# Two quarters of the modulation summed on VectorE and GpSimd before TensorE closes them

## The chip, the core and the metric

The kernel runs on one core of one Trainium2 chip. The metric is the device time of one execution in microseconds. Before the change the median of three runs is 1029.71 us (1029.26 to 1030.7). Engine names are those of the profile: PE is TensorE (PEld its weight loads), DVE is VectorE, ACT is ScalarE, POOL is GpSimd, SP is SyncE, which issues most of the DMAs.

## The reference, cut to what matters

One layer of a diffusion transformer, all in float32: 1024 latent tokens (`x`), 256 context tokens (`ctx`), width 1024. Only its beginning is touched:

```python
mod_x = (silu(c) @ w_mod + b_mod)        # one row of 6*1024 for the latents
mod_c = silu(c_ctx) @ w_mod + b_mod      # one row for the context tokens
sh1, sc1, ... = split(mod_x, 6);  csh1, csc1, ... = split(mod_c, 6)
h_x = rmsnorm(x, g_pre_mix) * (1 + sc1) + sh1       # 1024 x 1024
h_c = rmsnorm(ctx, g_pre_mix) * (1 + csc1) + csh1   # 256 x 1024
u_x = h_x @ w_in[:, :512]                           # pool part; then q, k, v, attention, output, MLP
```

Shift and scale of the first sub-layer are a product of a vector of 1024 with a 1024 x 2048 part of `w_mod`, for two vectors at once: silu(c) and silu(c_ctx).

## The kernel before, in words

Products are kept near float32 by splitting each operand into a high part (fp32r) and a low part (what is left), and summing three matmuls: high by high, low by high, high by low. ACT makes the high part and DVE the low part (`high_low`, L181, through L146 or L148 and L152 or L154; `modulated`, L202, with L205 to L210).

The beginning (`startup`, all five engines in the order in which the program is written, by `in_order`, L104) goes in four quarters q of the width, each of 256 columns of shift and 256 of scale, which are two blocks k = 2q and 2q + 1 of 128 rows of the transposed latents `xT`:

- SP loads in this order: eight pages of `x`; then for each quarter four pages of `w_mod` of 512 KB (`mod_load`, L297, issue at L300: K half by shift or scale, each 128 partitions x 4 blocks of K x 256 columns) and the raw rows of `w_in` (`wu0` to `wu3`, L178); then the context tokens. The pages come from a pool of 33, and SP waits only for a DMA eight places earlier.
- `mod_rows(q)` (L409) sums the quarter's modulation on PE: for each of the 8 blocks k of K and each of shift and scale, one matmul of 32 columns of `sT` (column 0 is silu(c), column 1 silu(c_ctx), the rest zero) with 256 columns of `w_mod` (L401), in four column groups of 32 of one bank `pm`: groups 0 and 1 take shift and scale of even k, groups 2 and 3 those of odd k. That is 16 matmuls, 32 records in the profile. ACT copies `pm` to `mrow` (L406).
- `shift_scale(q, mr)` (L415): four records of a small matmul with a constant `pck` turn the rows into columns and add the two halves (L418, `pmt`); DVE adds the bias and multiplies by the gain (L422 to L427, for the latents v = 0 and the context v = 1).
- `latents(q)` (L458) makes `hx`, the modulated latents, high and low, for two halves b of the tokens and the two blocks k: ACT L208, DVE L209 and L210 for b = 0; ACT L205 and L206, DVE L210 for b = 1.
- `some_sums(b, js, k)` (L444, matmuls at L449) adds block k of K to the sums `pu` of the pool part: 12 matmuls for b = 0 and 6 for b = 1 (the other 6 follow later).

The loop over q (the lines that the diff changes stand in it) has for q < 3: the sums of b = 0 with k = 2q, `mod_rows(q + 1)`, the split of the next weights `wu(q + 1)`, the sums of b = 0 with k = 2q + 1, `shift_scale(q + 1)`, the sums of b = 1 with both k, `latents(q + 1)`. So the PE work between the end of `mod_rows` and the first use of the new quarter hides the copy, the turn into columns, the scales and the first `hx`.

GpSimd has nothing to do between the eight reciprocal roots of the token norms (L140, each an operation of one element in a partition) and the two of the context tokens at the end of q = 2. Its other work in the kernel, which the prediction uses for prices, are the attention tables (L885) and a few splits (L896 and L897); L1374, L1387 and L136 to L140 are the norms of a later stage.

Of the kernel before, what the change touches and what calls it, by code (L numbers as in the profile page):

```python
# [11 lines left out]
F32 = mybir.dt.float32  # L12
# [6 lines left out]
P = 128  # L19
D = 1024  # L20
# [60 lines left out]
def hybrid_block(ctx, tc, x, ctx_in, w_mod, b_mod, gp1, gp2, w_in, pool_w, rpb, w_out, w1, w2, vectors,  # L81
                 mask, edge, out):
    nc = tc.nc
    sub, mul, add = ALU.subtract, ALU.mult, ALU.add
# [8 lines left out]
    def cst(name, shape, dt=F32):  # L93
        return const.tile(shape, dt, tag=name, name=name)
# [4 lines left out]
    def page(name, dt=F32):  # L99
        return act.tile([P, 1024], dt, tag="pg", name=name)  # L100
# [75 lines left out]
    def load(name, src):  # L176
        raw = wraw.tile([P, 1024], F32, tag="raw", name=f"{name}w")
        nc.sync.dma_start(raw.rearrange("p (a b) -> p a b", b=src.shape[-1]), src)  # L178
        return raw

    def high_low(name, raw, factor=1.0):  # L181
        hi = whl.tile([P, 1024], F32R, tag="hl", name=f"{name}h")
        lo = whl.tile([P, 1024], F32R, tag="hl", name=f"{name}l")
        split(raw, hi, lo, factor)
        return hi, lo
# [4 lines left out]
    def pair(w, kk, c0, n):  # L190
        return w[2 * kk * P : (2 * kk + 2) * P, c0 : c0 + n].rearrange("(a p) f -> p a f", p=P)

    def wk(w, k, lo, c, n):
        return w[k // 2][lo][:, (k % 2) * 512 + c : (k % 2) * 512 + c + n]
# [70 lines left out]
    def lasting(name):  # L265
        return ps_t.tile([P, 512], F32, tag="T", name=name)
# [4 lines left out]
    with tc.tile_pool(name="ps1", bufs=6, space=PSUM) as ps1, tc.tile_pool(name="tmp1", bufs=3) as tmp:  # L271

        def bank(name):
            if name[:2] == "pm" or name in ("pxt1_0", "pxt0_2", "pxt1_7", "pct2", "pct3"):
                return lasting(name)
            return ps1.tile([P, 512], F32, tag="mm", name=name)

        def once(name, shape):
            return tmp.tile(shape, F32, tag=name, name=name, bufs=1)
# [11 lines left out]
        def token_tile(name, src):  # L291
            t = page(name)
            nc.sync.dma_start(t, src)
            return t


        def mod_load(q, kh, w):  # L297
            src = w_mod[:, w * D + q * 256 : w * D + (q + 1) * 256].rearrange("(h k p) f -> h p k f", p=P, h=2)
            t = page(f"wm{q}_{kh}_{w}")
            nc.sync.dma_start(t.rearrange("p (k f) -> p k f", k=4), src[kh])  # L300
            return t

        xn = [token_tile(f"x{n}", x[n * P : (n + 1) * P, :]) for n in range(NT)]
        wm, raw_u = [], []
        for q in range(4):
            wm.append([[mod_load(q, kh, w) for w in range(2)] for kh in range(2)])
            raw_u.append(load(f"wu{q}", pair(w_in, q, 0, 512)))
        cp = [token_tile(f"c{i}", ctx_in[i * P : (i + 1) * P, :]) for i in range(2)]

# [4 lines left out]
        sT = once("sT", [P, KT, 32])  # L314
# [12 lines left out]
        def squares(name, t):  # L327
            jk = page(f"jk{name}")
            ms = sm(f"ms_{name}", 1, 4)
            mean_square(jk, t, ms)  # L330
            inverse[name] = rsqrt_of(f"t_{name}", ms)

        def normalised(name, t):
            nc.vector.tensor_scalar_mul(t, t, inverse[name])
# [59 lines left out]
        s1 = [cst(f"s1{v}", [P, KT]) for v in range(2)]  # L394

        def mod_sums(q, pm, kh):
            for k in range(4 * kh, 4 * kh + 4):
                for w in range(2):
                    c = 2 * (k % 2) + w
                    o = (k % 4) * 256  # L400
                    nc.tensor.matmul(pm[32 * c : 32 * c + 32, :256], sT[:, k, :], wm[q][kh][w][:, o : o + 256],  # L401
                                     start=(k < 2), stop=(k >= KT - 2))

        def mod_kept(q, pm):
            mr = tmp.tile([P, 256], F32, tag="mrow", name=f"mrow{q}", bufs=2)
            nc.scalar.copy(mr, pm[:, :256])  # L406
            return mr

        def mod_rows(q):  # L409
            pm = bank(f"pm{q}")  # L410
            for kh in range(2):
                mod_sums(q, pm, kh)
            return mod_kept(q, pm)

        def shift_scale(q, mr):  # L415
            pt = bank(f"pmt{q}")
            for j in range(2):
                nc.tensor.matmul(pt[:, 4 * j : 4 * j + 4], mr[:, j * P : (j + 1) * P], pck, start=True, stop=True)  # L418
            pv = pt[:, :8].rearrange("p (j w v) -> p w v j", w=2, v=2)
            hs = slice(2 * q, 2 * q + 2)  # L420
            for v in range(2):
                nc.vector.tensor_tensor(a1[v][:, hs], pv[:, 1, v], b_sc[:, hs], add)  # L422
                nc.vector.tensor_tensor(a1[v][:, hs], a1[v][:, hs], g1c[:, hs], mul)
                if q < 2:
                    nc.vector.tensor_tensor(s1[v][:, hs], pv[:, 0, v], b_sh[:, hs], add)
                else:
                    nc.vector.scalar_tensor_tensor(s1[v][:, hs], pv[:, 0, v], -1.0, b_sh[:, hs], mul, sub)  # L427
# [16 lines left out]
        def some_sums(b, js, k):  # L444
            h = hx[b][k]
            hi, lo = h[:, :512], h[:, 512:]
            for n, (low, r) in enumerate(((0, hi), (1, hi), (0, lo))):
                for j in js:
                    nc.tensor.matmul(pus[b][j], wk(wgt, k, low, j * P, P), r,  # L449
                                     start=(k == 0 and n == 0), stop=(k == KT - 1 and n == 2))  # L450
# [7 lines left out]
        def latents(q):  # L458
            for b in range(2):
                for k in (2 * q, 2 * q + 1):  # L460
                    latent(b, k)
# [5 lines left out]
        pm = bank("pm0")  # L467
        for kh in range(2):
            mod_sums(0, pm, kh)
        mr = mod_kept(0, pm)  # L470
        nc.scalar.copy(wu0h, raw_u[0])
        wgt.append((wu0h, wu0l))
# [10 lines left out]
        for q in range(4):  # L483
            some_sums(0, range(4), 2 * q)
            if q == 0:
                some_sums(0, (0, 1), 1)
            if q < 3:
                mr = mod_rows(q + 1)
                wgt.append(high_low(f"wu{q + 1}", raw_u[q + 1], 1.0 if q == 0 else -1.0))
            some_sums(0, range(2 if q == 0 else 0, 4), 2 * q + 1)  # L490
            if q < 3:
                shift_scale(q + 1, mr)
            for k in (2 * q, 2 * q + 1):
                some_sums(1, range(2), k)
            if q < 3:
                latents(q + 1)
            if q == 2:
                for i, t in enumerate(cp):
                    squares(f"c{i}", t)
                for i, t in enumerate(cp):  # L500
                    normalised(f"c{i}", t)
# [59 lines left out]
        for k in range(KT):  # L561
            for i in range(2):
                o = (k % 2) * 256 + i * P
# [392 lines left out]
        with in_order(ET.PE, ET.Pool, ET.Activation, ET.DVE, ET.SP) as pooling:  # L956
            banks = {of: [bank(f"p{of}{j}") for j in range(2)] for of in "KQ"}
            use(-1)
            for step, (n, of, j) in enumerate([(n, of, j) for n, of in products for j in range(2)]):
                half_product(n, of, j, banks[of])  # L960
                use(step)
                if step in (5, 9, 17):
                    name = {5: "S1", 9: "S4", 17: "S3"}[step]
# [4 lines left out]
                if step in (7, 11):  # L968
                    name = {7: "S4", 11: "S3"}[step]
# [19 lines left out]
    with (  # L989
# [4 lines left out]
        bank = lasting  # L994
# [178 lines left out]
        def halves_of(name):  # L1173
            both = [page(f"{name}{i}") for i in range(2)]
            return [both[t // 2][:, (t % 2) * 512 : (t % 2) * 512 + 512] for t in range(4)]
# [17 lines left out]
        with in_order(ET.PE, ET.Activation, ET.DVE, ET.SP) as projected:  # L1193
# [27 lines left out]
            for i in range(N + 4):  # L1221
# [48 lines left out]
                else:  # L1270

                    t = i - N
                    if t == 0:
                        x, s1 = [], halves_of("so1_")
# [51 lines left out]
    with tc.tile_pool(name="ps2", bufs=6, space=PSUM) as ps2:  # L1326
# [6 lines left out]
      with ExitStack() as tmp2:  # L1333
        tmp = tmp2.enter_context(tc.tile_pool(name="tmp2", bufs=4))
# [20 lines left out]
        def out_bank_sums(name, a, w):  # L1355
            ps = [bank(f"{name}_{t}") for t in range(4)]
            for t in range(4):
                out_sums(ps[t], a, w, t, True)
            return ps
# [32 lines left out]
        with tc.issue_after(projected[ET.DVE]), tc.issue_after(projected[ET.Activation]), in_order(ET.Activation, ET.DVE) as added:  # L1392
# [20 lines left out]
            v = out_bank_sums("pov", "S3", wt3)  # L1413
            c = {}
# [484 lines left out]
        with tc.issue_after(first[ET.PE]), in_order(ET.PE, ET.Activation, ET.DVE, ET.SP):  # L1899
# [3 lines left out]
            tmp = tmp2.enter_context(tc.tile_pool(name="tmp3", bufs=4))  # L1903

            def four(name):
                return [bank(f"{name}_{t}") for t in range(4)]

            def halves(name):
                both = [page(f"{name}{i}") for i in range(2)]
                return [both[t // 2][:, (t % 2) * 512 : (t % 2) * 512 + 512] for t in range(4)]  # L1910
# [19 lines left out]
            def half(m, h):  # L1930
                return rows[m][:, h * 512 : (h + 1) * 512]
# [37 lines left out]
            s1 = halves("s1")  # L1969
# [15 lines left out]
            v, z = four("pyv"), four("pyz")  # L1985
# [10 lines left out]
            for g in range(NG // 2):  # L1996
                group(v, "P4", g, more=True, last=(g == NG // 2 - 1))
                group(z, "P3", g, more=True)
                c = half(4 + g, 1)
# [53 lines left out]
```

## Time and profile before

| what | value |
|---|---|
| median of three runs | 1029.71 us |
| profiled execution, its own time | 1031.34 us |
| its span on the core | 1029.6 us |
| mean granted TensorE clock | 0.996 |
| PE busy | 1014.6 us, 99% |
| DVE busy | 747.1 us, 73% |
| ACT busy | 546.8 us, 53% |
| POOL busy | 142.6 us, 14% |

The profile is that of one execution. A row of the timeline gives the start in us from the beginning of the span, the duration, the engine, the line of the kernel, the operation, output and inputs with their shapes, how many instructions are merged in it, and in square brackets how long the engine had been idle and what ended that. A row of groups gives the busy time in us and the mean duration of one instruction in ns. A row of the windows gives the length of the stretch, the busy time of PE, PEld, DVE, ACT and POOL with their instructions, the granted TensorE clock, the share of the DMA engines and GB/s.

### The profile page before, as it was taken

Reading aid. Unit: us, or ns where it says so; the run is one execution under the profiler, and the core shown is the slowest. Engines: PE = TensorE matmul, PEld = TensorE weight load, DVE = VectorE, ACT = ScalarE, POOL = GpSimd, SP = SyncE. Lnnn points to the kernel's source line nnn. Section 1 sums busy time; section 2 is a strip of 40 time slices with the busy share of each in tenths; the row PEclk is TensorE's granted clock in tenths of the full one; section 3 lists DMA queues with packets and bytes.
Section 4 is the critical chain, followed back from the end, with each engine's and each line's share of the span. In section 5 each row is a group of like instructions: output and inputs, shape, how many; then the busy total and the mean of one; then the engine's idle time right before and its main releaser. Section 6 shows DMA issues by size and latency. Waiting matters only on the chain.

```text
span 1029.6 us, 16022 instructions
## 1 busy us (share of the span) xinstructions
PE 1014.6 (99%) x5910; PEld 840.7 (82%) x5910; DVE 747.1 (73%) x1160; ACT 546.8 (53%) x945; POOL 142.6 (14%) x225
## 2 busy tenths in 40 slices
PE   8999999999999999999999999999999999999997
PEld 7788888878898788888888888888888888888885
DVE  5588757857886687878998888755766666556576
ACT  7573254338897556776655554545543334334431
POOL 3011110126774311410000000000000000000001
PEclk9999999999999999999999999999999999999999
DMA  9999798623338966785776667537967766556556
GB/s 343 333 255 338 248 257 303 204 48 97 74 94 215 214 180 190 262 229 186 260 262 202 216 204 230 189 123 242 337 218 263 254 222 220 201 183 190 172 185 210
DMA packets 123134, 222.70 MB, mean 216 GB/s; under 512 B 9456, under 2 KB 55152, under 8 KB 123056
## 3 DMA queue, kind: packets, MB, share of 16 engines
q1 hardware_dynamic: 96560, 171.14, 50.6%
q0 software_dynamic: 9360, 19.58, 9.4%
q10 hardware_dynamic: 17136, 30.97, 8.1%
q8 instruction: 46, 0.75, 0.3%
q14 instruction: 32, 0.26, 0.1%
HBM read 168.16 MB, written 52.45 MB: 214 GB/s over the span
## 4 chain that ended last, share of the span: by engine, by line
PE 94%; DMA 2%; DVE 1%; issue 0%; ACT 0%; POOL 0%; SPq 0%; DVEq 0%; POOLq 0%; ACTq 0%
PE pu L449 4%; PE pa L1098 4%; PE S L1018 3%; PE phz L198 3%; PE phv L198 3%; PE phx L198 3%; PE pyx L198 3%; PE phx L200 3%; PE pyx L200 3%; PE phz L200 3%; PE pyx L199 3%; PE pyv L198 3%; PE pyz L199 3%; PE pyv L199 3%; PE phv L200 3%; PE pyz L198 3%
## 5 line engine op out<-in xcount | busy, mean ns | idle before, releaser
L1044 ACT ACTIVATE sp<-sp,nm 128x640 f32<-128x640 f32 (+1 forms) x64 | 51.5, 804 | 11.4 <-DVE nm L1033 5.3
L1033 DVE CUSTOM_DVE_ANT_0 sp<-S,tab 128x640 f32<-128x640 f32 (+1 forms) x56 | 44.5, 795 | 14.2 <-PE pz L1064 10.3
L1639 ACT ACTIVATE c<-c 128x512 f32<-128x512 f32 x48 | 30.3, 631 | 44.8 <-DVE c L1759 25.7
L146 ACT CAST wpS<-S 128x512 fp32r<-128x512 f32 x64 | 38.8, 616 | 27.4 <-PE phv L200 9.5
L198 PE MATMUL phx<-thB,wpA 128*128 128x512 f32 x128 | 50.2, 392 | 0.0
L200 PE MATMUL phx<-thB,wpA 128*128 128x512 f32 x128 | 49.8, 389 | 0.0
L199 PE MATMUL phx<-tlB,wpA 128*128 128x512 f32 x128 | 49.8, 389 | 0.0
L152 DVE TENSOR_TENSOR wpS<-S,wpS 128x512 fp32r<-128x512 f32 x64 | 43.4, 685 | 7.4 <-ACT wpS L146 7.4
L140 POOL TENSOR_TENSOR ry<-vy,nhalf 128x1 f32<-128x1 f32 x8 | 5.9, 740 | 281.5 <-DVE vy L138 281.5
L1640 ACT ACTIVATE c<-c 128x512 f32<-128x512 f32 x48 | 30.3, 630 | 15.6 <-DVE sa L1722 12.1
L198 PEld LDWEIGHTS phx<-thB,wpA 128*128 128x128 f32 x128 | 24.0, 188 | 5.4 <-ACT s L1690 0.5
L200 PEld LDWEIGHTS phx<-thB,wpA 128*128 128x128 f32 x128 | 24.0, 188 | 5.1
L199 PEld LDWEIGHTS phx<-tlB,wpA 128*128 128x128 f32 x128 | 24.0, 188 | 4.8
L1098 PE MATMUL pa<-pt,v 128*64 128x128 f32 x352 | 25.9, 280 | 0.2
L1083 DVE COPY pt<-T 128x512 f32<-128x512 f32 x32 | 21.9, 686 | 5.6 <-PE T L1064 5.6
L198 PE MATMUL phz<-thB,wpS 128*128 128x512 f32 x64 | 25.0, 391 | 0.0
L198 PE MATMUL phv<-thT,wpA 128*128 128x512 f32 x64 | 25.0, 391 | 0.0
L199 PE MATMUL phz<-tlB,wpS 128*128 128x512 f32 x64 | 24.9, 390 | 0.0
L199 PE MATMUL phv<-tlT,wpA 128*128 128x512 f32 x64 | 24.9, 389 | 0.0
L200 PE MATMUL phz<-thB,wpS 128*128 128x512 f32 x64 | 24.9, 389 | 0.0
L199 PE MATMUL phy<-tlT,wpS 128*128 128x512 f32 x64 | 24.9, 389 | 0.0
L200 PE MATMUL phy<-thT,wpS 128*128 128x512 f32 x64 | 24.9, 389 | 0.0
(1133 smaller groups left out, 3431.8 us busy)
## 6 DMA issues: line engine op xcount, KB each, us to landing
b<-in_w SPq DMA_DIRECT2D x64, 512.0 KB, 4.6
hrS<-hdS SPq DMA_DIRECT2D x32, 512.0 KB, 5.0
hrA<-hdA SPq DMA_DIRECT2D x24, 512.0 KB, 5.8
wm<-in_w_mod SPq DMA_DIRECT2D x16, 512.0 KB, 9.8
wa_0w<-in_w SPq DMA_DIRECT2D x16, 512.0 KB, 5.0
wa_1w<-in_w SPq DMA_DIRECT2D x16, 512.0 KB, 4.4
hdA<-c ACTq DMA_DIRECT2D x32, 256.0 KB, 2.9
hdS<-sa ACTq DMA_DIRECT2D x32, 256.0 KB, 3.2
```

Source lines behind the costliest of these rows:

```text
L146: nc.scalar.copy(hi, src)
L152: nc.vector.tensor_tensor(lo, src, hi.bitcast(F32), sub)
L198: nc.tensor.matmul(ps, ahi, bhi, start=first, stop=False, skip_group_check=more)
L199: nc.tensor.matmul(ps, ahi, blo, start=False, stop=False, skip_group_check=more)
L200: nc.tensor.matmul(ps, alo, bhi, start=False, stop=last, skip_group_check=more)
L449: nc.tensor.matmul(pus[b][j], wk(wgt, k, low, j * P, P), r, start=(k == 0 and n == 0), stop=(k == KT - 1 and n == 2))
L1018: nc.tensor.matmul(S[e][:, c0 : c0 + k[0].shape[1]], q[n_q][hs, cols], k[n_k][hs], start=(n_q + n_k == 0), stop=(n_q == 1))
L1033: nc.vector.tensor_tensor_reduce(out=to, in0=s, in1=bt, scale=1.0, scalar=BIG, op0=add, op1=ALU.min, accum_out=nm)
L1044: nc.scalar.activation(sp, sp, AF.Exp, bias=least[i, e], scale=-1.0, accum_out=sums[i][:, e : e + 1])
L1098: nc.tensor.matmul(pa[e * HD : (e + 1) * HD, cols], v[:, f : f + HD], turns[i][:, e, c] if c < 4 else fifths[i][:, :, (e + 1) * HD : (e + ...
L1639: nc.scalar.activation(r, src, AF.Relu)
L1640: nc.scalar.activation(r, r, AF.Square)
```

## The change

Quarters 0 and 1 stay as they are. For quarters 2 and 3:

- the weights come as four pages by blocks of K (two blocks each, shift and scale side by side), each in two DMAs of 256 KB (`mod_pairs`), so 8 DMAs of 256 KB in a quarter instead of 4 of 512 KB;
- blocks 0 to 5 of K are multiplied by silu(c) on DVE and by silu(c_ctx) on GpSimd, and added there over the blocks, all 128 partitions apart, shift and scale in one operation of 512 columns (`mod_added`): DVE does one `tensor_scalar_mul` and five `scalar_tensor_tensor`, GpSimd six `tensor_scalar_mul` and five `tensor_tensor` in a quarter;
- PE closes the sum (`mod_closed`): four matmuls for blocks 6 and 7 and four that sum the two added tiles over the partitions with a constant `pick`, eight instead of 16;
- in the loop, blocks 0 and 1 of quarter 2 are added in q = 0 ahead of the split of `wu1`; in q = 1 blocks 2 to 5 of quarter 2 and 0 and 1 of quarter 3 stand ahead of the split of `wu2`; in q = 2 blocks 2 to 5 of quarter 3 stand ahead of the split of `wu3`. `mod_closed` stands behind the sums of b = 0 with k = 2q + 1, where `mod_rows` stood ahead of them, and half of the sums of b = 1 (k = 2q) moves between `mod_closed` and `shift_scale`.

```diff
+        def mod_pairs(q, h):
+            t = page(f"wm{q}_{h}")
+            to = t.rearrange("p (k w f) -> w p k f", k=2, w=2)
+            for w in range(2):
+                src = w_mod[h * 2 * P : (h + 1) * 2 * P, w * D + q * 256 : w * D + (q + 1) * 256]
+                nc.sync.dma_start(to[w], src.rearrange("(k p) f -> p k f", p=P))
+            return t
...
-            wm.append([[mod_load(q, kh, w) for w in range(2)] for kh in range(2)])
+            wm.append([[mod_load(q, kh, w) for w in range(2)] for kh in range(2)] if q < 2 else
+                      [mod_pairs(q, h) for h in range(4)])
...
+        pick = once("pick", [P, 2, 32])
+        nc.gpsimd.memset(pick, 0.0)
+        for v in range(2):
+            nc.gpsimd.memset(pick[:, v, v : v + 1], 1.0)
+        added = {}
+
+        def mod_added(q, ks):
+            if q not in added:
+                added[q] = [tmp.tile([P, 512], F32, tag="t", name=f"md{q}_{v}", bufs=7) for v in range(2)]
+            for k in ks:
+                w = wm[q][k // 2][:, (k % 2) * 512 : (k % 2) * 512 + 512]
+                s0, s1 = (sT[:, k, v : v + 1] for v in range(2))
+                if k == 0:
+                    nc.vector.tensor_scalar_mul(added[q][0], w, s0)
+                    nc.gpsimd.tensor_scalar_mul(added[q][1], w, s1)
+                else:
+                    nc.vector.scalar_tensor_tensor(added[q][0], w, s0, added[q][0], mul, add)
+                    more = tmp.tile([P, 512], F32, tag="t", name=f"mm{q}_{k}", bufs=7)
+                    nc.gpsimd.tensor_scalar_mul(more, w, s1)
+                    nc.gpsimd.tensor_tensor(added[q][1], added[q][1], more, add)
+
+        def mod_closed(q):
+            pm = bank(f"pm{q}")
+            for k in range(2):
+                for w in range(2):
+                    c, o = 2 * k + w, (2 * k + w) * 256
+                    nc.tensor.matmul(pm[32 * c : 32 * c + 32, :256], sT[:, 6 + k, :], wm[q][3][:, o : o + 256],
+                                     start=True, stop=False)
+            for v in range(2):
+                for w in range(2):
+                    c = 2 * v + w
+                    nc.tensor.matmul(pm[32 * c : 32 * c + 32, :256], pick[:, v, :], added[q][v][:, w * 256 : w * 256 + 256],
+                                     start=False, stop=True)
+            return mod_kept(q, pm)
...
             some_sums(0, range(4), 2 * q)
             if q == 0:
                 some_sums(0, (0, 1), 1)
+            if q == 0:
+                mr = mod_rows(q + 1)
+            elif q < 3:
+                mod_added(q + 1, range(2, 6))
+            if q < 2:
+                mod_added(q + 2, range(2))
             if q < 3:
-                mr = mod_rows(q + 1)
                 wgt.append(high_low(f"wu{q + 1}", raw_u[q + 1], 1.0 if q == 0 else -1.0))
             some_sums(0, range(2 if q == 0 else 0, 4), 2 * q + 1)
+            if q in (1, 2):
+                mr = mod_closed(q + 1)
+                some_sums(1, range(2), 2 * q)
             if q < 3:
                 shift_scale(q + 1, mr)
-            for k in (2 * q, 2 * q + 1):
+            for k in (2 * q, 2 * q + 1) if q in (0, 3) else (2 * q + 1,):
                 some_sums(1, range(2), k)
```

The added tiles `md` and the products `mm` share the seven 512-wide slots of tag `t` with the first two `hx` temporaries.

## The prediction

> **What bounds the kernel now.** I read the page first (shares, then the chain that ended last), then the chain, the waits and the windows of the beginning.
>
> ```profile
> span 1029.6 us, 16022 instructions
> PE 1014.6 (99%) x5910; PEld 840.7 (82%) x5910; DVE 747.1 (73%) x1160; ACT 546.8 (53%) x945; POOL 142.6 (14%) x225
> ...
> PE 94%; DMA 2%; DVE 1%; issue 0%; ACT 0%; POOL 0%; SPq 0%; DVEq 0%; POOLq 0%; ACTq 0%
> ```
>
> PE is busy 99% of the span and carries 94% of the chain, so what PE does later or longer in the beginning comes out at the end one to one, unless a later wait for something that does not move gives it back. The stretch of the change, cut from the chain, and the only DMA wait among PE's waits:
>
> ```profile
> 37.01 1.86 PE pm L401 x32
> 38.87 2.95 PE pu L449 x12
> 41.82 0.34 PE pmt L418 x4
> 42.16 5.59 PE pu L449 x24
> 47.75 1.86 PE pm L401 x32
> ```
>
> ```profile
> PEld pm L401 <- DMA wm<-in_w_mod: 0.2, 1, 0.2
> ```
>
> And the stretch in the windows:
>
> ```profile
> 23.20:76.40 53.20, 53.20 (x316) 41.79 (x317) 37.77 (x76) 35.96 (x61) 4.39 (x4) 1.00 0.96 296
> ```
>
> PE works without a gap from 23.2 to 76.4 us; a matmul of `some_sums` costs 5.59 / 24 = 0.233 us there, a round of modulation 1.86 us. DVE is busy 37.8 of those 53.2 us and POOL 4.4. After this stretch PE waits for no DMA, only for engines that follow PE's own work, so I take no part of a delay as given back.
>
> **The change part by part.**
>
> *Removed from PE.* Two rounds of 16 matmuls become two of 8: 2 x 1.86 / 2 = 1.86 us less. This is the whole possible gain.
>
> *Added to DVE and POOL, priced alone.* The nearest rows with the same shape, all operands in SBUF:
>
> ```profile
> L210 DVE TENSOR_TENSOR hx<-xT,hx 128x512 fp32r<-128x512 f32 x14 | 9.4, 690 | 1.4 <-ACT hx L206 1.1
> L209 DVE TENSOR_SCALAR xT<-xT,a,s 128x512 f32<-128x512 f32 x6 | 3.3, 544 | 1.7 <-ACT hx L208 1.7
> L423 DVE TENSOR_TENSOR a<-a,cols 128x2 f32<-128x2 f32 x8 | 1.3, 161 | 0.3
> L154 DVE SCALAR_TENSOR_TENSOR mix<-y,mix 128x512 fp32r<-128x512 f32 x4 | 2.6, 684 | 0.0
> L896 POOL CAST qP<-q 128x512 fp32r<-128x512 f32 x4 | 2.4, 612 | 0.0
> L897 POOL TENSOR_TENSOR qP<-q,qP 128x512 fp32r<-128x512 f32 x4 | 5.2, 1290 | 0.3
> ```
>
> DVE in a quarter: one multiplication at 0.544 (L209) and five `scalar_tensor_tensor` at 0.684 (L154), 3.96 us. POOL: five additions at 1.290 (L897), and six multiplications, whose form has no row. They lie between the one-input cast, 0.612, and the two-input addition, 1.290; I take 0.61, because one tensor comes in as with the cast, and keep 1.29 for the range. That makes 6 x 0.61 + 5 x 1.29 = 10.1 us, against a period of 10.7 us (37.01 to 47.75). Alone, each engine would just keep up. They are not alone.
>
> *DVE and POOL shut each other out.* The rows that decide, from the timeline and the groups:
>
> ```profile
> 203.59 0.45 POOL L885 TENSOR_TENSOR tab<-msk,U0w 128x128 f32<-128x128 f32 x1
> 203.60 1.53 DVE L154 SCALAR_TENSOR_TENSOR wQT4l<-wQT4w,wQT4h 128x1024 fp32r<-128x1024 f32 x1 [0.18 <-ACT wQT4h L148]
> 204.01 1.43 POOL L885 TENSOR_TENSOR tab<-msk,U0w 128x128 f32<-128x128 f32 x1
> L885 POOL TENSOR_TENSOR tab<-msk,U 128x128 f32<-128x128 f32 x36 | 15.1, 450 | 0.0
> L154 DVE SCALAR_TENSOR_TENSOR wu3l<-wu3w,wu3h 128x1024 fp32r<-128x1024 f32 x1 | 1.2, 1225 | 3.4 <-ACT wu3h L148 3.4
> 7.21 0.76 DVE L334 TENSOR_SCALAR x<-x,rt_x 128x1024 f32<-128x1024 f32 x1
> 6.13 0.55 POOL L140 TENSOR_TENSOR rt_x<-vt_x,nhalf 128x1 f32<-128x1 f32 x1 [4.61 <-DVE vt_x L136]
> 7.36 1.02 POOL L140 TENSOR_TENSOR rt_x<-vt_x,nhalf 128x1 f32<-128x1 f32 x1 [0.68 <-DVE vt_x L136]
> ```
>
> A DVE operation with two SBUF inputs, 1.225 us elsewhere, takes 1.53 when it starts just behind a POOL operation; the next POOL operation takes 1.43 instead of 0.45 and ends at 205.44, 0.31 us behind DVE's end at 205.13. So they go one after the other. Behind a DVE `TENSOR_SCALAR` (7.21 to 7.97) the POOL root takes 1.02 instead of 0.55. Of the 0.45 us of the POOL operation, DVE waited 1.53 - 1.225 = 0.31; 0.13 us of each POOL operation are therefore free, and I count the rest as exclusive.
>
> The Trainium skill, SBUF — State Buffer, section "SBUF: two separate sides", says the same of the port pair that the two share, but has the holder keep it for the whole instruction; by that the 22 POOL operations would hold 2.9 us more and the time would be 1049. The 0.31 of 0.45 us here speaks for the smaller value.
>
> *The ledger.* From the landing of quarter 2's first page to POOL's last addition of quarter 3, these operations exclude each other:
> - DVE: the added sums, 2 x 3.96 = 7.92; `latents` of quarters 1 and 2, each 2 x 0.544 (L209) + 4 x 0.690 (L210), 7.70 in all; the low halves of `wu1` to `wu3`, 3 x 1.225 = 3.68 (`wu3`'s follows DVE's last sum at once and so comes ahead of POOL's last addition; 1.2 less if it does not); four gain products at 0.161 (L423), 0.64. Sum 19.9.
> - POOL: in a quarter 6 x (0.61 - 0.13) + 5 x (1.29 - 0.13) = 8.7; two, 17.4.
>
> Together 37.3 us. One of the two always has such an operation ready: when DVE waits for `pmt` or `hx`, POOL still has its chain, and POOL waits for nothing but pages, its own results and slots. (POOL's multiplications for blocks 4 and 5 of quarter 3 also wait until PE has read quarter 2's tiles, which is earlier.) The start:
>
> ```profile
> 21.27 2.01 SPq L300 DMA_DIRECT2D wm<-in_w_mod  x1
> wm<-in_w_mod SPq DMA_DIRECT2D x1, 512.0 KB, 9.9
> ```
>
> This is quarter 2's first page; bytes and order of the queue stay the same, so the new first page (two DMAs) lands at about 21.27 + 9.9 = 31.2 as well; the engines start at 31.3. POOL's last addition ends at 31.3 + 37.3 = 68.6.
>
> *From there to PE's restart.* PE then has the last two pick matmuls (1.86 / 8 = 0.23), six moved matmuls (1.40), `pmt` (0.34) and six more (1.40): 72.0. The chain beside it (the three rows between serve further down):
>
> ```profile
> 32.04 0.15 DVE L422 TENSOR_TENSOR a<-pmt,cols 128x2 f32<-128x2 f32 x1
> 32.49 1.52 ACT L208 ACTIVATE hx<-xT,s,a 128x512 fp32r<-128x512 f32 x2 [1.63 <-DVE s L425]
> 34.12 1.07 PE L449 MATMUL pu<-hx,wu1h 128*128 128x512 f32 x4
> 36.78 0.69 DVE L210 TENSOR_TENSOR hx<-xT,hx 128x512 fp32r<-128x512 f32 x1 [0.38 <-ACT hx L206]
> 30.90 1.23 DVE L152 TENSOR_TENSOR wu1l<-wu1w,wu1h 128x1024 fp32r<-128x1024 f32 x1 [2.63 <-ACT wu1h L146]
> 55.62 1.07 PE L449 MATMUL pu<-hx,wu3h 128*128 128x512 f32 x4
> ```
>
> From DVE's scale to the first `hx` it is 32.49 - 32.04 + 1.52 / 2 = 1.2 us, just covered by the last six matmuls (1.40); before, twelve covered it, so that cover is used up. Before, PE began quarter 3's sums at 55.62. The delay is 72.0 - 55.6 = 16.4 us, with the saved 1.86 already in it, since PE waits for the closing anyway. Half-way the same ledger has on DVE quarter 2's sums (3.96), the first two blocks of quarter 3 (1.23), one `latents` (3.85), two low halves (2.45) and two gain products (0.32), on POOL one quarter (8.7): 20.5 us, so quarter 2 closes at about 52 instead of 37.01 + 1.86 = 38.9.
>
> *Edits with small or no cost.* The first two added blocks stand in DVE's queue from 30.90 - 2.63 = 28.3 until the page lands; queued behind them are `wu1`'s low half and quarter 1's scales. Without any exclusion, scales that came at 32.04 would come at 31.3 + 0.54 + 0.68 + 1.23 = 33.7, and PE, whose sums of k = 2 began at 34.12, 0.9 us after their `hx` (32.49 + 0.76), would stop 0.8 us. In the ledger this is contained. SP issues eight more DMAs; the bytes are the same, PE's whole wait for these pages was 0.2 us, and now they are needed later: nothing. If the smaller DMAs left the queue thin, the start at 31.3 would move with the landing; a late us there is a late us in the ledger. ACT's high parts of `wu2` and `wu3` come ahead of the `mrow` copy, which waits for PE anyway. The three memsets of `pick` fall into POOL's idle time.
>
> *Sum.* Profiled execution: 1031.34 + 16.4 = 1047.7. It lies 1.6 above the median of the runs, so the forecast is 1029.7 + 16.4 = 1046.1. Two corrections I leave out, since they cancel: DVE's rows overlap by some 0.07 us (32.04 begins before the row that ends at 30.90 + 1.23), about 25 times, -1.7; and the clock (rival 4 has the rows), +1.7 for the second of two gaps; behind the first, PE's loss is hidden while POOL works through its second chain. The windows that show it:
>
> ```profile
> 218.00:221.00 3.00, 2.12 (x12) 1.47 (x12) 2.91 (x6) 1.97 (x4) 0.40 (x1) 1.00 1.02 175
> 221.00:224.00 3.00, 2.28 (x16) 1.77 (x15) 3.00 (x6) 1.87 (x4) 0.00 (x0) 0.79 0.66 169
> 224.00:227.00 3.00, 3.00 (x9) 2.11 (x8) 2.68 (x7) 1.50 (x4) 0.00 (x0) 0.64 0.01 3
> ```
>
> **The rivals.**
>
> 1. *No exclusion for these forms* (the other side). Then the 0.8 us stop, and a wait at each closing for DVE, which starts the last four blocks only behind `latents` (36.78 + 0.69 + 1.6 + 4 x 0.684 = 41.8, where PE arrives at 34.9 + 5.59 + 0.46 = 41.0), eat the gain: +0.1 to +0.9, 1030. With none of these waits it is -1.86, 1027.9. It decides where exclusion adds under 1 us a quarter. Against it: the rows at 203.6.
> 2. *Exclusion only between two-input operations.* Seen directly are POOL's two-input operations. If POOL's multiplications pass freely, 12 x 0.48 = 5.8 us go, 1040.3; if DVE's six tensor-scalar operations too, 3.3 more, 1037. Against it: the rows at 7.21 and 7.36.
> 3. *POOL multiplies as slowly as it adds*: 12 x 0.68 = 8.2 more, 1054.3. For it: no row of the form.
> 4. *The clock falls in both gaps.* In the rows above PE worked 4.4 of 6 us, and the clock then fell to 0.79 and 0.64, (0.21 + 0.36) x 3 = 1.7 us lost. Here PE stands almost still for some 9 us (it is through k = 3 at about 43, and quarter 2 closes at 52) and 7 us (52 + 3.4 + 5.6 + 0.5 = 61.5 to 68.6). With neither loss hidden it is 2 x 1.7 more, 1049.5. The Trainium skill, TensorE: Matmul & The Clock Gate, Part 1, gives half rate after an idle window of about 3.4 us; the rows above, with no such idle window, fall earlier.
>
> **How the numbers follow.** Chances: the ledger 0.50 (own range 1042 to 1050), rival 1 0.14, rival 2 0.15, rival 3 0.10, rival 4 0.11. About 0.2% (2.1 us) can be told from no change. Faster is rival 1 without its waits, helped by chance: 0.03; the rest of it is the same, 0.11; all else is slower, 0.86. The range goes from rival 2's lower end, less 1, to rival 3's end: 1036 to 1055; below it lies rival 1.
>
> **What would show it.** Right: POOL and DVE rows between 31 and 69 us with 1 us and more in place of 0.61 and 0.68; PE waits for POOL at both closings, near 52 and 69 us; a falling clock behind them. Wrong: POOL's rows stay at 0.61 and 1.29, PE's closings lie near 42 and 52, and the sums of quarter 3 begin near 55.6 us; or DVE alone, not POOL, is the last at the closings.

## The result and the profile after

The changed kernel takes 1049.4 us (median of 5 runs, 1048.7 to 1050.06) against 1029.83 us before (median of 5): the ratio is 1.0187, with a 95% interval of 1.0176 to 1.0199. It is slower by 19.6 us. The forecast was 1046.1 us within 1036 to 1055.

The page of the changed kernel: the span, the busy times and the shares of the chain that ended last.

```profile
span 1047.4 us, 16021 instructions
...
PE 1018.6 (97%) x5878; PEld 840.8 (80%) x5878; DVE 766.0 (73%) x1172; ACT 545.8 (52%) x945; POOL 179.3 (17%) x250
...
PE 91%; POOL 4%; SPq 2%; DVE 1%; DMA 1%; issue 1%; ACT 0%; POOLq 0%; DVEq 0%; ACTq 0%
```

PE has 32 instructions fewer and yet 4 us more busy time; POOL, which was no part of the chain before, has 4% of it. This is the chain from 15 to 95 us: start, length, what.

```profile
by line: PE pu L493 28.5%; POOL mm L431 24.3%; POOL md L432 16.0%; DMA wm<-in_w_mod 9.7%; SPq L300 5.2%; POOL md L427 4.2%; SPq L178 4.1%; issue 3.0%; PE pct L616 2.2%; PE pm L444 1.3%; SPq L308 0.9%; PE pmt L462 0.8%; POOLq L431 0.1%; POOL
...
31.07 1.85 POOL md L427
...
67.32 1.50 POOL md L432
...
68.87 1.07 PE pm L444 x4
69.93 2.86 PE pu L493 x6
72.79 0.65 PE pmt L462 x4
73.44 12.65 PE pu L493 x54
```

From the landing of the first page to 68.82 us every piece of the chain is POOL's (or the issue of its next operation). Then six matmuls take 2.86 us, which take 1.40 at full clock, and `pmt` 0.65 instead of 0.34. PE's waits, and its rows at the two closings and at the first sums of quarters 2 and 3 (k = 4 and k = 6):

```profile
PE pm L444 <- DVE md L429: 7.4, 2, 3.8
PE pm L444 <- POOL md L432: 3.8, 1, 3.8
```

```profile
46.20 0.84 PE L444 MATMUL pm<-md,pick 128*32 128x256 f32 x4 [3.75 <-DVE md L429]
50.86 1.07 PE L444 MATMUL pm<-md,pick 128*32 128x256 f32 x4 [3.83 <-POOL md L432]
...
57.41 1.09 PE L493 MATMUL pu<-hx,wu2h 128*128 128x512 f32 x4
...
67.75 2.19 PE L444 MATMUL pm<-md,pick 128*32 128x256 f32 x8 [3.66 <-DVE md L429]
...
75.00 1.09 PE L493 MATMUL pu<-hx,wu3h 128*128 128x512 f32 x4
```

Quarter 3's sums began at 55.62 us before and begin at 75.00 now, 19.4 us later, and no later wait gives any of it back. The clock in three windows of that stretch (the value right behind the five engines' busy times):

```profile
48.00:51.00 3.00, 0.14 (x2) 0.14 (x4) 1.69 (x2) 0.00 (x0) 2.92 (x3) 0.50 0.08 20
...
69.00:72.00 3.00, 3.00 (x9) 1.81 (x9) 0.90 (x1) 0.37 (x1) 0.00 (x0) 0.50 0.31 64
72.00:75.00 3.00, 3.00 (x13) 2.52 (x12) 0.90 (x7) 1.06 (x2) 0.00 (x0) 0.70 0.86 253
```

What POOL does for these 37.7 us, as groups (28 to 80 us) and as single rows:

```profile
L431 POOL TENSOR_SCALAR mm<-wm,sT 128x512 f32<-128x512 f32 x10 | 19.6, 1956 | 0.0
L432 POOL TENSOR_TENSOR md<-md,mm 128x512 f32<-128x512 f32 x10 | 14.1, 1412 | 0.8
L427 POOL TENSOR_SCALAR md<-wm,sT 128x512 f32<-128x512 f32 x2 | 3.4, 1703 | 14.5 <-DMA wm<-in_w_mod 14.5
```

```profile
50.79 1.56 POOL L427 TENSOR_SCALAR md<-wm,sT 128x512 f32<-128x512 f32 x1
52.33 1.56 POOL L431 TENSOR_SCALAR mm<-wm,sT 128x512 f32<-128x512 f32 x1
53.97 1.27 POOL L432 TENSOR_TENSOR md<-md,mm 128x512 f32<-128x512 f32 x1
55.22 1.56 POOL L431 TENSOR_SCALAR mm<-wm,sT 128x512 f32<-128x512 f32 x1
...
61.29 2.52 POOL L431 TENSOR_SCALAR mm<-wm,sT 128x512 f32<-128x512 f32 x1
...
67.32 1.49 POOL L432 TENSOR_TENSOR md<-md,mm 128x512 f32<-128x512 f32 x1
```

From 50.79 to 55.47 us DVE waits for `pmt`, so these rows show POOL alone. A multiplication takes 1.56 us there, not the 0.61 of the prediction, and a block of multiplication and addition comes every 55.22 - 52.33 = 2.89 us. Two quarters at this pace are 2 x (1.54 + 5 x 2.89) = 32.0 us. POOL needed 68.81 - 31.07 = 37.7, so 5.7 us are what POOL loses beside DVE (2.52 at 61.29 instead of 1.56 is one such row). DVE's side of the meeting:

```profile
31.52 1.06 DVE L429 SCALAR_TENSOR_TENSOR md<-wm,sT,md 128x512 f32<-128x512 f32 x1
...
35.23 1.57 DVE L209 TENSOR_SCALAR xT<-xT,a,s 128x512 f32<-128x512 f32 x1 [0.55 <-ACT hx L208]
...
63.40 4.29 DVE L429 SCALAR_TENSOR_TENSOR md<-wm,sT,md 128x512 f32<-128x512 f32 x4
```

The first runs from its start to its end inside POOL's multiplication of 31.07 to 32.92; the second starts together with POOL's addition of 35.23 and takes 1.57 instead of 0.544, 1.03 more. So an addition holds DVE off for most of its length; a multiplication does so only for a small part (the first row against the 0.75 that DVE takes alone, below: 0.31). The third row is DVE's last sum: it ended at 67.69, only 1.1 us ahead of POOL's last addition, so at the second closing DVE is nearly as late as POOL.

### The profile page after: what moved, and what is told of

Its sections match the earlier page's. It is cut to its first block, busy times and chain, and to the rows that moved or that the text cites. A ratio compares the mean times of both kernels' runs of the same rounds, so it can differ in the third digit from the quotient of the medians.

```text
span 1047.4 us, 16021 instructions
## 1 busy us (share of the span) xinstructions
PE 1018.6 (97%) x5878; PEld 840.8 (80%) x5878; DVE 766.0 (73%) x1172; ACT 545.8 (52%) x945; POOL 179.3 (17%) x250
## 4 chain that ended last, share of the span: by engine, by line
PE 91%; POOL 4%; SPq 2%; DVE 1%; DMA 1%; issue 1%; ACT 0%; POOLq 0%; DVEq 0%; ACTq 0%
PE pa L1150 3%; PE S L1070 3%; PE phv L198 3%; PE phz L198 3%; PE phx L198 3%; PE pyx L198 3%; PE pyv L200 3%; PE pyx L200 3%; PE pyz L200 3%; PE phx L200 3%; PE pyz L199 3%; PE pyv L199 3%; PE phx L199 3%; PE phz L199 3%; PE phv L199 3%; PE phv L200 3%
## 5 line engine op out<-in xcount | busy, mean ns | idle before, releaser
L198 PE MATMUL phv<-thT,wpA 128*128 128x512 f32 x64 | 25.0, 391 | 0.0
L200 PE MATMUL phv<-thT,wpA 128*128 128x512 f32 x64 | 24.9, 389 | 0.0
```

Of the source, the lines that this page charges most:

```text
L198: nc.tensor.matmul(ps, ahi, bhi, start=first, stop=False, skip_group_check=more)
L200: nc.tensor.matmul(ps, alo, bhi, start=False, stop=last, skip_group_check=more)
```

## The experiments

Two theories stood at the start. The *ledger* is the prediction's: DVE and POOL exclude each other, and the sum of both sets the closings, whatever its parts. The *chain* theory came from the rows above: POOL's own slow chain sets the closings, and DVE only delays it by 5.7 us. The table has all runs, each time beside that of the kernel before on the same chip; "sums" is the start of quarter 3's sums in the profile (55.62 before).

| kernel | us | before | ratio (95%) | sums |
|---|---|---|---|---|
| changed kernel | 1049.4 | 1029.83 | 1.0187 (1.0176 to 1.0199) | 75.00 |
| order and loads alone | 1030.9 | 1029.86 | 1.0009 (1.0 to 1.0017) | 55.78 |
| both sums left out | 1053.68 | 1030.65 | 1.0224 (1.0209 to 1.024) | 78.89 |
| both left out, pages kept | 1029.05 | 1030.2 | 0.9988 (0.9979 to 0.9997) | 54.05 |
| no context sum (POOL) | 1032.27 | 1029.86 | 1.0022 (1.0014 to 1.0031) | 57.07 |
| no latent sum (DVE) | 1048.47 | 1029.86 | 1.0176 (1.0163 to 1.019) | 74.55 |
| PE kept busy, both gaps | 1049.05 | 1029.86 | 1.0188 (1.0174 to 1.0202) | 77.12 |
| PE kept busy, second gap | 1047.98 | 1030.06 | 1.0174 (1.016 to 1.0187) | 74.09 |
| POOL copies | 1043.07 | 1030.06 | 1.0123 (1.0109 to 1.0137) | 68.22 |
| POOL multiplies two tensors | 1048.1 | 1030.06 | 1.0173 (1.016 to 1.0187) | 73.70 |
| ACT multiplies | 1043.8 | 1030.06 | 1.0135 (1.0121 to 1.0149) | 68.79 |
| DVE makes both sums | 1039.42 | 1030.65 | 1.0088 (1.0071 to 1.0105) | 64.18 |

The profiled execution of "PE kept busy, both gaps" took 1051.9 us, 2.9 above its median, so its start of the sums is that much late; in the other rows the start less 55.62 agrees with the difference of the medians within 1 us.

### The order and the loads alone

```diff
-            for k in range(2):
+            for k in range(KT):
                 for w in range(2):
-                    c, o = 2 * k + w, (2 * k + w) * 256
-                    nc.tensor.matmul(pm[32 * c : 32 * c + 32, :256], sT[:, 6 + k, :], wm[q][3][:, o : o + 256],
-                                     start=True, stop=False)
-            for v in range(2):
-                for w in range(2):
-                    c = 2 * v + w
-                    nc.tensor.matmul(pm[32 * c : 32 * c + 32, :256], pick[:, v, :], added[q][v][:, w * 256 : w * 256 + 256],
-                                     start=False, stop=True)
+                    c, o = 2 * (k % 2) + w, (2 * (k % 2) + w) * 256
+                    nc.tensor.matmul(pm[32 * c : 32 * c + 32, :256], sT[:, k, :], wm[q][k // 2][:, o : o + 256],
+                                     start=(k < 2), stop=(k >= KT - 2))
...
-                mod_added(q + 1, range(2, 6))
+                pass
...
-                mod_added(q + 2, range(2))
+                pass
```

> Loads by pairs and the new place of the closing kept, but PE sums all eight blocks itself (16 matmuls), nothing added on VectorE or GpSimd. If the new order and the smaller DMAs cost nothing (the last six matmuls, 1.4 us, cover the 1.2 us from the scale to the first hx): 1029.8, within 0.7. If the used-up cover or a thinner DMA queue counts: 1031 to 1033, with PE waits for hx or for wm.

It costs 1.0 us by the medians (1030.9 against 1029.86, interval 0 to 1.8 us) and 0.2 us by the start of the sums. The pages in two DMAs and the moved matmuls are not where the 19 us are.

### Both sums left out

```diff
-                added[q] = [tmp.tile([P, 512], F32, tag="t", name=f"md{q}_{v}", bufs=7) for v in range(2)]
+                added[q] = [wm[q][3][:, :512], wm[q][3][:, 512:]]
...
-                    nc.vector.tensor_scalar_mul(added[q][0], w, s0)
-                    nc.gpsimd.tensor_scalar_mul(added[q][1], w, s1)
...
-                    nc.vector.scalar_tensor_tensor(added[q][0], w, s0, added[q][0], mul, add)
-                    more = tmp.tile([P, 512], F32, tag="t", name=f"mm{q}_{k}", bufs=7)
-                    nc.gpsimd.tensor_scalar_mul(more, w, s1)
-                    nc.gpsimd.tensor_tensor(added[q][1], added[q][1], more, add)
```

> Both added sums are left out, on DVE and on POOL; the closing rounds read a weight page in their place, so quarters 2 and 3 of the modulation lack three quarters of K. It measures the gain alone, half of two rounds on PE, 1.86 us by the prediction. If the gain is whole: 1028.2 (before 1030.0 less 1.86), and the sums of quarter 3 begin 1.9 us earlier than the 55.62 of before, at 53.8. If the changed order (PE's moved matmuls behind the closing, the pages in two DMAs) eats it: 1029.5 to 1030.5.

It fell outside both, at 1053.68 us, for a reason of its own. DVE's copies of the turned latents wait for a weight page:

```profile
30.30 0.69 DVE L362 COPY xT<-pxt 128x512 f32<-128x512 f32 x1 [16.27 <-DMA wm<-in_w_mod]
```

Three pages of each of the two quarters had no reader left. Their places in the pool of pages went to `xT` tiles, which then had to wait for the loads into them. So this run says nothing on the sums. The next one gives every page a reader:

```diff
-                added[q] = [wm[q][3][:, :512], wm[q][3][:, 512:]]
+                added[q] = [wm[q][0][:, :512], wm[q][1][:, :512]]
...
-                    nc.tensor.matmul(pm[32 * c : 32 * c + 32, :256], sT[:, 6 + k, :], wm[q][3][:, o : o + 256],
+                    nc.tensor.matmul(pm[32 * c : 32 * c + 32, :256], sT[:, 6 + k, :], wm[q][2 + k][:, w * 256 : w * 256 + 256],
```

> As the run before, both added sums left out, but the closing rounds read all four weight pages of their quarter (one for the latents' pick matmuls, one for the context's, two for the blocks 6 and 7), so no page is given to another tile ahead of its load. If the gain is whole: 1028.2 (before 1030.1 less 1.86), and the sums of quarter 3 begin at about 53.8. If the changed order eats it: 1029.5 to 1030.5.

```profile
54.05 1.20 PE L489 MATMUL pu<-hx,wu3h 128*128 128x512 f32 x4
```

This is the gain when both sums cost nothing: 1.15 us by the medians (interval 0.3 to 2.2), 55.62 - 54.05 = 1.57 us in the trace, of the 1.86 that PE saves. With this order and these loads it is all that summing elsewhere can win.

### The latents' sum alone, and the context's sum alone

POOL's part taken out:

```diff
-                added[q] = [tmp.tile([P, 512], F32, tag="t", name=f"md{q}_{v}", bufs=7) for v in range(2)]
+                added[q] = [tmp.tile([P, 512], F32, tag="t", name=f"md{q}", bufs=7), wm[q][3][:, :512]]
...
-                    nc.gpsimd.tensor_scalar_mul(added[q][1], w, s1)
...
-                    more = tmp.tile([P, 512], F32, tag="t", name=f"mm{q}_{k}", bufs=7)
-                    nc.gpsimd.tensor_scalar_mul(more, w, s1)
-                    nc.gpsimd.tensor_tensor(added[q][1], added[q][1], more, add)
```

> GpSimd's part left out: the context's sums of quarters 2 and 3 are not made, PE closes with a page of weights in their place, so the context's shift and scale come out wrong. VectorE's part stays. All theories that put the loss on GpSimd, by its own time or by exclusion: 1030 to 1031, closings near 42 and 52 us, clock at full. If VectorE's queue alone carries part of it: above 1033.

DVE's part taken out:

```diff
-                added[q] = [tmp.tile([P, 512], F32, tag="t", name=f"md{q}_{v}", bufs=7) for v in range(2)]
+                added[q] = [wm[q][3][:, :512], tmp.tile([P, 512], F32, tag="t", name=f"md{q}", bufs=7)]
...
-                    nc.vector.tensor_scalar_mul(added[q][0], w, s0)
...
-                    nc.vector.scalar_tensor_tensor(added[q][0], w, s0, added[q][0], mul, add)
```

> VectorE's part left out: the latents' sums of quarters 2 and 3 are not made, PE closes with a page of weights in their place, so their shift and scale come out wrong. GpSimd's part stays. Ledger theory (all exclusive operations add up): 7.9 us fewer, about 1041.5. Chain theory (GpSimd's own multiplications and additions, 1.56 and 1.29 us, 32 of the 37.7 us, set the closings and exclusion only adds some 5): 2 to 4 us fewer, 1045.5 to 1047.5.

Without POOL's part 17 of the 19.6 us are gone, and the closings lie at 42.0 and 53.1 us. The 1032.27 us fall between the two values expected (up to 1031, or above 1033): a small part is DVE's own. Against the kernel without any sum the start of quarter 3's sums moves from 54.05 to 57.07, 3.0 us, of which 2.3 are new waits of PE (1.8 at the closings, 0.5 for `hx`; the other 0.4 us for `hx` stand in the kernel before too). PE's waits from 20 to 70 us:

```profile
PE pm L440 <- DVE md L428: 1.8, 2, 1.0
PE pu L489 <- ACT hx L208: 0.9, 2, 0.5
```

Without DVE's part only 0.9 us are gone, no more than the noise. The ledger wanted 7.9, so it falls as it was put. The chain theory wanted 2 to 4 and missed too. Rows of POOL in the kernel without the latents' sum:

```profile
45.56 1.26 POOL L430 TENSOR_TENSOR md<-md,mm 128x512 f32<-128x512 f32 x1
46.80 1.56 POOL L429 TENSOR_SCALAR mm<-wm,sT 128x512 f32<-128x512 f32 x1
...
60.95 3.05 POOL L429 TENSOR_SCALAR mm<-wm,sT 128x512 f32<-128x512 f32 x1
```

POOL has its own pace for long stretches, but its two chains still take 37.1 us (31.10 to 68.22), 5.1 more than alone. It now meets DVE's other work at another place: twice a multiplication starts at the end of `latents` and runs through DVE's low half of the next weights (at 40.03 and 61.44 us), and takes 3.05 us instead of 1.56. So what POOL loses beside DVE, 5.7 us in the changed kernel, hardly hangs on DVE's sums.

### PE kept busy through the gaps

```diff
+            spare(pm[:, 384:], 72 if q == 2 else 44)
             for k in range(2):
```

`spare` issues that many small PE transposes whose result nobody reads, ahead of each closing; in the second kernel 46 ahead of the second closing alone.

> The changed kernel, with 72 and 44 transposes of the identity into unused columns of the bank ahead of the two closings, so that PE does not stand still while it waits. If the fallen clock costs the 3 us between 72.0 and 75.0 us: clock 1.0 throughout, 1046.4. If it costs nothing because PE waits anyway: 1049.4.

> The changed kernel with 46 transposes of the identity only ahead of the second closing, where PE otherwise stands from 64 to 69 us. If the clock lost behind the second gap is a term of its own (2.86 us for six matmuls in place of 1.40, 0.65 for the small ones in place of 0.34, 1.07 for the picks in place of 0.5): full clock from 69 us on, PE's restart about 2.5 us earlier, 1047. If it is not on the path: 1049.4.

In the first kernel the spare work ended at 65.9 us, POOL at 70.32, and PE's clock fell (0.63 from 69 to 72 us, 0.50 from 72 to 75); nothing was won (1049.05). That the first gap's loss was gone as well (quarter 2's sums began at 55.28 instead of 57.41) won nothing either: POOL's second chain hides it, as the prediction says. In the second kernel PE was busy up to 69.35 us, and the clock was 1.00 from 57 to 78 us:

```profile
70.17 0.63 PE L445 MATMUL pm<-md,pick 128*32 128x256 f32 x4 [0.82 <-POOL md L432]
...
74.09 1.20 PE L494 MATMUL pu<-hx,wu3h 128*128 128x512 f32 x4
```

From the closing to quarter 3's sums it is 3.9 us here, 6.1 in the changed kernel (68.87 to 75.00): the clock behind the second gap costs 2.2 us. The start of the sums moved by 0.9 only, since POOL was 1.3 us later in this execution, 0.6 of it from a later page (it starts at 31.66). The medians differ by 1.4 us, which alone is near the noise; the clock's price is read from the trace.

### Cheaper multiplications

Three kernels change the multiplications only. The first copies the block instead, the second gives GpSimd the scalar as a tensor, spread over the 512 columns, the third multiplies on ACT and leaves GpSimd the additions. The multiplication of block 0 changes likewise.

```diff
-                    nc.gpsimd.tensor_scalar_mul(more, w, s1)
+                    nc.gpsimd.tensor_copy(more, w)
```

> GpSimd's twelve multiplications replaced by copies of the same tiles (the scale is left out, so the context's shift and scale come out wrong); additions, VectorE's part and order stay. Copies of this size take 0.61 us, the multiplications take 1.56. Chain theory (GpSimd's own time sets the closings): up to 12 x 0.95 = 11.4 us fewer until VectorE's sums and the exclusion take over, 1037 to 1042. Ledger theory (exclusive shares, equal for a copy and a multiplication, about 0.4 us each): no change, 1048 to 1050.

```diff
-                    nc.gpsimd.tensor_scalar_mul(more, w, s1)
+                    nc.gpsimd.tensor_tensor(more, w, s1.to_broadcast([P, 512]), mul)
```

> GpSimd's multiplications written as a product of two tensors, the second one column read 512 times; everything else as in the changed kernel. Chain theory: if this form costs what the additions cost, 1.29 us and not 1.56, the chain is 12 x 0.27 = 3.2 us shorter, 1046; but it holds VectorE off for some 1.0 us and not 0.4, which may take that back. Ledger theory: longer exclusive shares, 12 x 0.6 = 7 us more, 1056.

```diff
-                    nc.gpsimd.tensor_scalar_mul(more, w, s1)
+                    nc.scalar.activation(more, w, AF.Copy, scale=s1)
```

> The context's twelve multiplications on ScalarE, which has 4 of 10 us free in each quarter; GpSimd only adds (five of 1.29 us in a quarter). Chain theory: GpSimd's chain is 6.5 us in a quarter and no longer the last; VectorE's sums, held off by additions, and the copy of the row, queued behind six multiplications of 0.6 us on ScalarE, are: 1033 to 1037. Ledger theory: 12 x 0.4 = 5 us fewer, 1044.

With copies POOL is through at 58.3 us and DVE is the last at the second closing. The time, 1043.07, lies 1 us above what the chain theory wanted and 5 below the ledger's 1048. POOL's last block, and PE's row at the second closing:

```profile
56.23 0.61 POOL L431 COPY mm<-wm 128x512 f32<-128x512 f32 x1
56.92 1.34 POOL L432 TENSOR_TENSOR md<-md,mm 128x512 f32<-128x512 f32 x1
```

```profile
64.28 0.64 PE L444 MATMUL pm<-md,pick 128*32 128x256 f32 x8 [0.92 <-DVE md L429]
```

The price is the 0.61 of the prediction, so its own ledger can be held against this kernel: it wants quarter 3's sums at 72.0, and they start at 68.22. DVE worked here without idle time from 31.44 to 64.2, 32.8 us; at the pace that it has alone, in the last experiment, its list takes about 18.5 (sums 7.4, `latents` 7.4, two low halves 2.3, scales 1.4), so the 22 POOL operations held it off for 14.3. The ledger had 17.4.

With two-tensor multiplications it is the same: POOL is faster and DVE slower.

```profile
31.81 1.04 POOL L427 TENSOR_TENSOR md<-wm,sT 128x512 f32<-128x512 f32 x1 [14.89 <-DMA wm<-in_w_mod]
...
62.41 1.34 POOL L432 TENSOR_TENSOR md<-md,mm 128x512 f32<-128x512 f32 x1
```

```profile
69.77 0.64 PE L444 MATMUL pm<-md,pick 128*32 128x256 f32 x8 [0.88 <-DVE md L429]
```

A multiplication takes 1.04 us at the least, a third less than 1.56, and POOL ends at 63.8, 5 us earlier. DVE now ends at 69.7, against 67.7 in the changed kernel, and the time is 1048.1. DVE was busy from 31.77 to 69.7, 37.9 us, held off for 37.9 - 18.5 = 19.4. The ledger wanted 1056. The chain theory wanted 1046 and had named, without a price, that DVE may take it back. What both leave out is that the closing goes to whichever of the two engines is later.

On ACT, the multiplications of the last four blocks stand behind ACT's part of `latents` and start at 39.62; then DVE's sums and POOL's additions have only each other:

```profile
40.36 5.79 DVE L429 SCALAR_TENSOR_TENSOR md<-wm,sT,md 128x512 f32<-128x512 f32 x4
```

```profile
40.49 8.19 POOL L432 TENSOR_TENSOR md<-md,mm 128x512 f32<-128x512 f32 x5 [6.48 <-ACT mm L431]
```

Five additions in 8.19 us: they take turns with DVE every 1.64 us. DVE alone does such an operation every 0.66, so an addition of 1.27 holds it off for 0.98. The kernel still loses 13.7 us, where the chain theory had 1033 to 1037: PE waits 7.7 us at the closings, 1.6 us for the first `hx` (DVE's scales stand behind the low half of `wu1`, whose high part waits behind ACT's multiplications), and the clock falls behind both closings (0.71 from 48 to 51 us, 0.57 from 63 to 66). The ledger's number, 1044, is met here (1043.8). This does not bring the ledger back, after its misses of 5 to 8 us in three other kernels; but where POOL only adds, and so holds DVE off for most of each operation, a sum of both is nearly right.

### DVE makes both sums

```diff
-                    nc.gpsimd.tensor_scalar_mul(added[q][1], w, s1)
+                    nc.vector.tensor_scalar_mul(added[q][1], w, s1)
...
-                    more = tmp.tile([P, 512], F32, tag="t", name=f"mm{q}_{k}", bufs=7)
-                    nc.gpsimd.tensor_scalar_mul(more, w, s1)
-                    nc.gpsimd.tensor_tensor(added[q][1], added[q][1], more, add)
+                    nc.vector.scalar_tensor_tensor(added[q][1], w, s1, added[q][1], mul, add)
```

> DVE makes both added sums, the context's too (each block one more operation of DVE with its sum in it, 0.544 or 0.69 us), and POOL none; nothing is left out. By the theory that POOL's slow chain and the turns that it takes with DVE cost the time: DVE has 19.9 us and 7.9 for the context, 27.8, and 1.8 of small scale operations, from 31.3 on without much idle time, so its last sum ends at 59 to 61, quarter 3's sums begin at 62.5 to 64.5 and the time is 1036.5 to 1039, less than the changed kernel's 1049.4 although one engine does the work of two. By the theory that the added work itself is too much, wherever it is done: 1045 or more.

```profile
40.69 0.75 DVE L430 SCALAR_TENSOR_TENSOR md<-wm,sT,md 128x512 f32<-128x512 f32 x1
41.35 0.75 DVE L429 SCALAR_TENSOR_TENSOR md<-wm,sT,md 128x512 f32<-128x512 f32 x1
```

```profile
44.90 1.73 PE L442 MATMUL pm<-md,pick 128*32 128x256 f32 x8 [2.55 <-DVE md L429]
...
59.59 1.29 PE L442 MATMUL pm<-md,pick 128*32 128x256 f32 x8 [2.49 <-DVE md L429]
```

One engine does the work of two and the kernel is 10 us faster than with both (1039.42 against 1049.4). The sums start where expected (64.18, within 62.5 to 64.5), the time is 0.4 us above the range; that the added work is too much wherever it is done (1045 or more) is ruled out. A block of the context costs DVE 0.66 us and costs POOL 2.89. The kernel is still 8.8 us slower than before: PE waits 5.0 us for DVE's sums at the closings and 1.1 us for the first `hx`, whose scales stand behind DVE's first sums, and the clock falls behind the first closing.

## Why the prediction was right, point by point

The direction and the total came out, 16.4 us against 19.6, and the end that the total rests on, POOL's last addition at 68.6 us, was measured at 68.8. The parts did not: two errors met, and that they nearly cancel is luck.

- *Removed from PE*, 1.86 us: measured alone as 1.15 (medians) to 1.57 (trace).
- *POOL's multiplication*, "I take 0.61, because one tensor comes in as with the cast". This step failed. The multiplication takes 1.56 us alone, more than both ends of the range for it (0.612 and 1.290): for 12 of them 11.4 us more. The copy, which has one input too, did take 0.61, so the number of inputs does not decide the price; the form does.
- *DVE and POOL shut each other out*, "0.13 us of each POOL operation are therefore free". The rows give 0.14 (0.45 - 0.31), which changes the sum by 0.2 us. That they shut each other out is right in kind, but the share is too high: additions hold DVE off for 0.98 of 1.27 us, copies for (14.3 - 10 x 0.98) / 12 = 0.38 of 0.61, the two-tensor multiplication for (19.4 - 9.8) / 12 = 0.8 of 1.04 (both by subtraction from a kernel's total), and the multiplication of the change for 0.31 in the row shown, of 1.56 that it takes alone. The Trainium skill, SBUF — State Buffer, section "SBUF: two separate sides", has an exclusive pair that the holder keeps for the whole instruction; here the part held depends on the form: by that one row it is about a fifth for the changed kernel's multiplication, and DVE's operation ended before POOL's did.
- *The ledger*. It adds what the two engines hold; but with a slow multiplication that holds little, POOL's own chain (32.0 us) is the longer, and DVE adds 5.7 to it (5.1 without DVE's sums). 37.7 against the ledger's 37.3 is chance. Where the price was as assumed, in the kernel with copies, the ledger is 3.8 us too long.
- *The two corrections left out*: the stretch behind the second closing is 6.18 - 3.37 = 2.8 us longer than the prediction's (68.82 to 75.00, against 68.6 to 72.0). The clock behind the second gap, put at 1.7, is 2.2 of it, which came back when PE was kept busy; the other 0.6 stay at full clock. The overlap of DVE's rows, which was to cancel the clock, was not measured; it would have to shorten POOL's chain, which is the longer one, to do so. This stretch is most of the 3 us between forecast and result. The first gap's loss was hidden, as said.
- *Edits with small or no cost*: order and loads cost 0.2 to 1.0 us, near nothing. The first added blocks ahead of the scales did stop PE, and with both closings DVE's part alone cost 3.0 us where rival 1 had waits of 2.0 to 2.8.
- *The rivals*. Rival 1 falls: POOL's part costs 17 us. Rival 2 had the right idea, multiplications that pass almost freely, but at 0.61 us. Rival 3 was nearest in the price (as slow as the addition; it is slower still), but added it whole to the ledger (1054.3). Rival 4 was right that the clock falls in both gaps (2.2 us for the second, where it had 1.7); that neither loss would be hidden was wrong.
- *What would show it*: PE waits at both closings near 52 and 69 us (50.86 and 68.87), with a falling clock behind them. "POOL, not DVE" held for the changed kernel, by 1.1 us at the second closing, and turned with the price of the multiplication. The sign of POOL rows of 1 us and more in place of 0.61 was met for another reason: the multiplication takes 1.56 us with DVE idle.

## What to carry to other kernels

Work that is spread over DVE and GpSimd has two prices, what each engine takes alone and what each holds the other off for, and the closing goes to the later engine: price both, and price the exact form of the instruction. If the form has no row, its nearest relatives need not bound it. Ask first what the gain can be at most (here 1.9 us of 1030) and what one engine alone would take: DVE alone does these sums in less time than DVE and GpSimd together, and even so loses 8.8 us.

## What the runs showed of the hardware

- GpSimd's multiplication by a scalar per partition takes 1.56 us for 128x512 float32, its product of two tensors, one of them spread from a column, 1.04, its copy 0.61.
- The faster of the two multiplications held DVE off longer (0.8 us by subtraction, against 0.3 in one row), and the two kernels came out 1.3 us apart.
- In the kernel where DVE makes both sums, PE stood still 2.55 us ahead of the first closing and 2.49 us ahead of the second, and the clock fell only behind the first:

```profile
45.00:48.00 3.00, 3.00 (x11) 1.42 (x11) 3.00 (x6) 0.37 (x1) 0.00 (x0) 0.51 0.91 339
...
60.00:63.00 3.00, 2.96 (x19) 2.03 (x17) 1.48 (x3) 0.37 (x1) 0.00 (x0) 1.00 0.13 35
```

The Trainium skill, TensorE: Matmul & The Clock Gate, Part 1, says that the activity window of about 3.4 us runs freely, and that the moment at which the clock changes depends on where in the window the first matmul lands. Two gaps of nearly one length with different outcomes would fit that, but no run here moves the gaps to test it. What the first one shows is that a gap of 2.55 us, shorter than such a window, can halve the clock.
